# Three feed-forwards of a transformer stack: one whole gate and up tile each instead of two

## Chip, cores and metric

One core of one Trainium2 chip. The metric is device time in microseconds (us) of one execution of the program; the kernel before takes 2332.36 us (median of 3 runs, 2330.86 to 2334.24). The profile is of a further execution of its own, which took 2334.35 us; its span, from the first to the last instruction, is 2332.6 us.

## What is computed

A stack of three blocks on 512 tokens (with 16 meta tokens, 528 columns), width 1024, all in fp32: a mixer with sparse attention and retention, a feed-forward, a mixer with stick-breaking attention, a feed-forward, and a block of four parallel branches with its own feed-forward. The change concerns the three feed-forwards. Cut to them, the reference is:

```
def conv_ffn(h, w_up, w_gate, conv_w, conv_b, w_down):
    u = h @ w_up
    g = h @ w_gate
    g = causal_conv_of_width_3(g, conv_w) + conv_b
    return (jax.nn.silu(g) * u) @ w_down

# in the last block, without the convolution
act = silu(h @ w_gate) * (h @ w_up)
x = x + act @ w_down
```

`w_gate` and `w_up` are 1024 x 2816, which makes 22 tiles of 128 columns each; `w_down` is 2816 x 1024.

## The kernel before, in words

**Layout.** The residual stream lies transposed in SBUF as eight tiles `hT[k]` of 128 x 528 (features by tokens). A projection makes one 128-column tile of the result at a time: the weights are the stationary operand, the tokens move. fp32 is emulated by three passes: weights and activations are split into a high part (a cast to fp32r) and a low part (the rest), and each product is three matmuls, high x high, high x low and low x high. The high part of weights is cast on ScalarE (in some helpers on VectorE if that is free first), the low part is a subtraction on VectorE.

**Whole tiles.** `proj` (L689) multiplies a weight tile of 128 x 8 x 128 with the eight activation tiles: 8 x 3 matmuls per column range. The first feed-forward has two ranges of 264 columns; the second has two of 258 for the gate and one of 512 for up; the third has one of 512 for both. `wtile` (L663) loads a tile (512 KB, issued on SyncE's queue) into one of three places `w_raw` and splits it into `w_hi` and `w_lo`. `prefetch` (L659) does so at the end of the stage before, for tiles that the feed-forward will take first.

**Block products.** The class `Fast` (L1147) takes a gate tile and an up tile together as a 2 x 2 block problem (two halves of the 1024 features, two halves of the tokens) and computes it with seven block products in place of eight: 7 x 4 x 3 = 84 matmuls of half the tokens (264, 258 or 256 columns). For that it needs

- four sums of the activations for each of four feature pairs, made once at the start of each feed-forward (`Fast.__init__`, L1150: tiles `th`, `tl`, with temporary tiles in the ring of raw weights);
- sums of the weights, for each pair of tiles anew (`blocks`, L1193): two loads of 512 KB, `s13` (1024 elements a row), `s24` (two operations of 512), and four splits, three of 1024 and one of 512;
- sums of the products, seven VectorE operations and one ScalarE copy per pair (`pair`, L1228).

The raw weights, the high parts and the low parts go through rings of five places each (three `w_...`, two `s_...`); the whole tiles use the `w_...` places of the same rings.

**The feed-forward.** `ffn` (L1253) and `block2_ffn` (L1881) go over the 22 tiles in groups (of 4, 4, 4, 4, 3, 3 and of 5, 5, 5, 4, 3). `gate_up(f)` (L1278, L1891) makes the activation tile `f`: whole where `f < FS`, by block products otherwise, then convolution (in the first two), Silu, product, and the split of the result into `ah` and `al`. From the second group on, the down projection of the group before is spread between the tiles. So the first group has no down projection beside it. `FS` is 2 (L45).

```
                if f < FS:
                    proj(pall, wtile(f"w_gu{l}", 2 * f), x, times(g[:, 2:], r), grange)
                elif f in WHOLE[l]:
                    ...
                else:
                    u = fp.tile([P, gw], F32, name="u", bufs=1)
                    fast.pair(f, g[:, 2:], u, r)
```

`WHOLE` is empty. `prepare` (L192) lays the weights out by the same constant: `w_gu*` holds the `2 * FS` whole tiles, `w_gs*` the paired blocks of all others.

**What sets the order.** Operations are recorded, not issued: `Order.record` (L444) collects them with their dependencies and a cost, and `Order.flush` (L514), called at the end of each stage, emits them as a greedy list schedule: at each step the engine that is free first takes its ready operation with the best priority. The priority is the place in the program less a weighted length of the path behind the operation (`RANK`, L371); weight preparation inside `early` and `wtile` is moved ahead by 500 places. Every engine runs its operations in the order emitted, and nothing crosses a flush. All instructions are recorded by helpers, so the profile gives them one line (L502), and they are told apart by the tiles' names.

Of the kernel before, what the change touches and what calls it, by code (L numbers as in the profile page):

```python
# [41 lines left out]
OSP = 3  # L42
BST = 0
OB = 2
FS = 2  # L45
WHOLE = ((), (), ())
HS = S // 2

# [2 lines left out]
def pack(w, tiles):  # L51

    kt = w.shape[0] // P
    out = np.zeros((len(tiles), P, kt, P), w.dtype)
    r = w.reshape(kt, P, w.shape[1]).transpose(1, 0, 2)
    for i, parts in enumerate(tiles):
        for at, c0, n in parts:
            out[i, :, :, at:at + n] = r[:, :, c0:c0 + n]
    return np.ascontiguousarray(out.reshape(len(tiles), P, kt * P))


def paired(a, b):

    h = a.shape[2] // 2
    return np.stack([np.concatenate([b[:, :, h:], a[:, :, :h]], 2), np.concatenate([b[:, :, :h], a[:, :, h:]], 2)], 1)


def whole(c0, n):
    return [[(0, c0 + P * i, P)] for i in range(n // P)]
# [122 lines left out]
def prepare(i):  # L192
# [7 lines left out]
    for l in range(2):  # L200
        g, u = pack(i["ffn_w_gate"][l], whole(0, DFF)), pack(i["ffn_w_up"][l], whole(0, DFF))
        a[f"w_gu{l}"] = np.stack([g[:FS], u[:FS]], 1).reshape(2 * FS, P, D)
        a[f"w_gs{l}"] = paired(g[FS:], u[FS:]).reshape(-1, P, D)
        for n, (f0, f1) in enumerate(GROUPS):
# [9 lines left out]
    g, u = pack(i["w_gate_2"][0], whole(0, DFF)), pack(i["w_up_2"][0], whole(0, DFF))  # L214
    a["w_gu2"] = np.stack([g[:FS], u[:FS]], 1).reshape(2 * FS, P, D)
    a["w_gs2"] = paired(g[FS:], u[FS:]).reshape(-1, P, D)
    for n, (f0, f1) in enumerate(GROUPS2):
# [376 lines left out]
def body(ctx: ExitStack, tc, A, out):  # L594
# [64 lines left out]
    def prefetch(name, *tiles):  # L659
        for i in tiles:  # L660
            fetched[name, i] = wtile(name, i)

    def wtile(name, i, kt=KD):  # L663
        if (name, i) in fetched:
            return fetched.pop((name, i))
        n = kt * P
        O.shift -= 500
        raw = wp.tile([P, D], F32, name="w_raw", bufs=3)
        if (name, i) == ("w_even", 0):
            O.boost = 3e6  # L670
        dma(raw[:, :n], A[name][i])
        O.boost = 0.0
        hi = wp.tile([P, D], F32R, name="w_hi", bufs=3)
        lo = wp.tile([P, D], F32R, name="w_lo", bufs=3)
        split(raw[:, :n], hi[:, :n], lo[:, :n])
        O.shift += 500
        return v2(hi, P), v2(lo, P)
# [71 lines left out]
    class Following:  # L749
# [9 lines left out]
        def add(self, m):  # L759
            src = hT[m][:, self.c0:]  # L760
            h, l = split_scaled(src, self.gain(m), xp, KD, self.w)
            self.x[0].append(h)
            self.x[1].append(l)
            add_square(self.acc, m == 0, src, *self.args)
            if self.gain2 is not None:
                add_square(self.acc2, m == 0, src, *self.args, gain=self.gain2(m))
# [8 lines left out]
    def follow(*a, **k):  # L775
        nxt_[0] = Following(*a, **k)
        return nxt_[0].add
# [73 lines left out]
    def even_mixer():  # L851
        with ExitStack() as es:
# [270 lines left out]
                    add(m)  # L1123
            for m in range(RF, KD):
                add(m)
            prefetch("w_gu0", 0, 1, 2)
            O.flush()


# [17 lines left out]
    class Fast:  # L1147
# [45 lines left out]
        def blocks(self, f):  # L1193


            i = f - FS
            r1, r2 = self.load(A[self.name][2 * i]), self.load(A[self.name][2 * i + 1])
# [16 lines left out]
        def tile(self, f, n, evac, x, ranges):  # L1214

            i = f - FS
            if n == 0:
# [110 lines left out]
    def odd_mixer():  # L1328
# [8 lines left out]
        with ExitStack() as es:  # L1337
# [19 lines left out]
            def out_proj(n, k0, k1, add=None):  # L1357
                for m in range(KD):
                    proj(pall if add else pd, wtile(f"w_oo_{n}", m, k1 - k0), (o_hl[0][k0:k1], o_hl[1][k0:k1]), add_h(m),
                         ((Q0, 270), (270, 528)), boost=0.0 if add else BST)  # L1360
                    if add:
                        add(m)
# [117 lines left out]
                o_hl[1].append(l_)  # L1480
            out_proj(0, 0, OSP)
            out_proj(1, OSP, KD, follow(lambda m: gcol(3, m), Q0, op, "otmp", 2))
            prefetch("w_gu1", 0, 1, 2)
            O.flush()


# [2 lines left out]
    def block2_mixer():  # L1489
        with ExitStack() as es:  # L1490
# [384 lines left out]
            for m in range(KD):  # L1875
                proj(pall, wtile("w_mg", m), mgx, add_h(m, NM), ONE)
                add(m)
            prefetch("w_gu2", 0, 1, 2)
            O.flush()

    def block2_ffn():  # L1881
        with ExitStack() as es:
# [38 lines left out]
            O.flush()  # L1921

    steps = [even_mixer, lambda: ffn(0, 1), odd_mixer, lambda: ffn(1, 3), block2_mixer, block2_ffn]
    for step in steps:
        step()
# [14 lines left out]
```

## Time and profile before

| what | us |
|---|---|
| median of 3 runs | 2332.36 |
| lowest and highest run | 2330.86, 2334.24 |
| the profiled execution | 2334.35 |
| its span | 2332.6 |
| TensorE busy in the span | 2288.6 |
| VectorE busy | 2004.4 |
| ScalarE busy | 1184.2 |
| the first feed-forward, about | 435 to 800 |
| the second | 1097 to 1440 |
| the third | 1982 to 2332 |

The profile is one execution on the chip. Matmuls overlap, so the time that one of them takes in a steady stream is the step from start to start, not its own duration. An engine's idle time is put down to the instruction on another engine, or the load, that came last before it went on. `w_hi`, `w_lo`, `s_hi`, `s_lo` are split weights, `xh`, `xl` split activations, `th`, `tl` their split sums, `sp`, `sv`, `u`, `g` and `y` the intermediate results of a tile; `d`, `at` and `pv` are PSUM.

### The profile page before, as it was taken

What the parts mean: (1) busy time and instruction counts of PE and PEld (TensorE: products, weight loads), DVE (VectorE), ACT (ScalarE), POOL (GpSimd) and SP (SyncE); (2) the same over time, 40 slices, a digit from 0 to 9 for tenths busy, and PEclk for the clock granted to TensorE, in tenths of its full rate; (3) what the DMA queues carried; (4) which work ended last, traced back from release to release, by engine and by line L of the source; (5) the groups of instructions that cost most, each with busy time, mean ns of one, the idle gap of its engine ahead of it and who ended that gap; (6) DMA issues with size and microseconds to landing.
All of it is one profiled execution on the core that took longest, in us unless ns stands there. A gap on an engine that the chain in (4) does not pass through costs nothing.

```text
span 2332.6 us, 39795 instructions
## 1 busy us (share of the span) xinstructions
PE 2288.6 (98%) x15488; PEld 2094.2 (90%) x15488; DVE 2004.4 (86%) x3975; ACT 1184.2 (51%) x2183; POOL 0.2 (0%) x4
## 2 busy tenths in 40 slices
PE   7999999999999999999999999899999999999999
PEld 7999999989999999999899998677888788899998
DVE  6999898899998889998999998676898776998886
ACT  4423556544444578886444445243677622543442
POOL 0000000000000000000000000000000000000000
PEclk9999999999999999999999999999999999999999
DMA  6222222222332311102332333222222122333332
GB/s 202 72 65 73 80 78 65 96 91 95 97 106 94 93 58 53 55 28 74 113 108 88 109 99 108 89 71 84 84 86 80 53 84 95 106 112 98 112 99 82
DMA packets 75774, 206.09 MB, mean 88 GB/s; under 512 B 8996, under 2 KB 20720, under 8 KB 75584
## 3 DMA queue, kind: packets, MB, share of 16 engines
q1 hardware_dynamic: 75584, 203.53, 27.4%
q8 instruction: 122, 2.00, 0.4%
q14 instruction: 68, 0.56, 0.1%
HBM read 201.37 MB, written 6.84 MB: 89 GB/s over the span
## 4 chain that ended last, share of the span: by engine, by line
PE 92%; DVE 5%; DMA 2%; issue 1%; ACT 1%; SPq 0%; ACTq 0%; DVEq 0%
PE d L502 51%; PE at L502 33%; PE pv L502 8%; DMA w_raw<-w_even 1%; DVE w_lo L502 1%; DVE w_raw L502 1%; DVE s_lo L502 1%; DVE y L502 0%; DMA w_raw<-w_gu 0%; DVE s_raw L502 0%; ACT w_hi L502 0%; DMA h<-h 0%; DVE tl L502 0%; DMA ob<-c_oh 0%; DMA s_raw<-w_gs 0%
## 5 line engine op out<-in xcount | busy, mean ns | idle before, releaser
L502 PE MATMUL d<-xh,w_hi 128*128 128x264 f32 (+4 forms) x1616 | 480.8, 325 | 12.6 <-ACT w_hi L502 7.8
L502 PE MATMUL d<-xl,w_hi 128*128 128x264 f32 (+4 forms) x1616 | 482.2, 326 | 1.1 <-DVE xl L502 1.0
L502 PE MATMUL d<-xh,w_lo 128*128 128x264 f32 (+5 forms) x1616 | 477.7, 324 | 0.0
L502 DVE TENSOR_TENSOR w_lo<-w_raw,w_hi 128x1024 fp32r<-128x1024 f32 (+5 forms) x322 | 320.6, 998 | 45.5 <-ACT w_hi L502 32.6
L502 ACT CAST w_hi<-w_raw 128x1024 fp32r<-128x1024 f32 (+5 forms) x239 | 206.4, 865 | 301.3 <-PE d L502 178.8
L502 PEld LDWEIGHTS d<-xh,w_hi 128*128 128x128 f32 x1616 | 291.5, 190 | 39.2 <-ACT w_hi L502 8.3
L502 PEld LDWEIGHTS d<-xl,w_hi 128*128 128x128 f32 x1616 | 291.5, 190 | 24.9 <-DVE xl L502 2.3
L502 PEld LDWEIGHTS d<-xh,w_lo 128*128 128x128 f32 x1616 | 290.3, 190 | 23.5 <-issue 1.9
L502 ACT CAST s_hi<-w_raw 128x512 fp32r<-128x512 f32 (+3 forms) x112 | 90.7, 812 | 89.6 <-PE at L502 38.5
L502 DVE CAST w_hi<-w_raw 128x1024 fp32r<-128x1024 f32 (+3 forms) x83 | 49.2, 593 | 73.6 <-PE d L502 62.9
L502 DVE TENSOR_TENSOR s_lo<-w_raw,s_hi 128x512 fp32r<-128x512 f32 (+3 forms) x112 | 103.3, 927 | 10.0 <-ACT s_hi L502 8.7
L502 PE MATMUL at<-xh,s_hi 128*128 128x264 f32 (+2 forms) x356 | 101.6, 286 | 3.3 <-DVE y L502 1.3
L502 ACT CAST w_hi<-s_raw 128x1024 fp32r<-128x1024 f32 (+3 forms) x76 | 63.1, 832 | 81.9 <-PE at L502 29.4
L502 PE MATMUL at<-xh,s_lo 128*128 128x264 f32 (+2 forms) x356 | 101.2, 284 | 0.0
L502 PE MATMUL at<-xl,s_hi 128*128 128x264 f32 (+2 forms) x356 | 101.2, 284 | 0.0
L502 ACT CAST s_hi<-s_raw 128x1024 fp32r<-128x1024 f32 (+3 forms) x74 | 62.9, 852 | 57.7 <-PE at L502 27.6
L502 ACT ACTIVATE e<-e,m 128x256 f32<-128x256 f32 (+4 forms) x142 | 76.5, 550 | 14.8 <-DVE m L502 13.5
L502 PE MATMUL d<-th,s_hi 128*128 128x264 f32 (+2 forms) x284 | 80.8, 285 | 2.8 <-DVE sp L502 2.3
L502 PE MATMUL d<-th,s_lo 128*128 128x264 f32 (+2 forms) x284 | 80.9, 285 | 2.5 <-DVE s_lo L502 2.4
L502 PE MATMUL at<-al,w_hi 128*128 128x264 f32 (+1 forms) x256 | 81.5, 335 | 0.0
L502 PE MATMUL at<-ah,w_hi 128*128 128x264 f32 (+1 forms) x256 | 81.4, 335 | 0.0
L502 PE MATMUL at<-ah,w_lo 128*128 128x264 f32 (+1 forms) x256 | 81.2, 334 | 0.0
(684 smaller groups left out, 6823.4 us busy)
## 6 DMA issues: line engine op xcount, KB each, us to landing
w_raw<-w_gs SPq DMA_DIRECT2D x71, 512.0 KB, 3.7
w_raw<-w SPq DMA_DIRECT2D x59, 512.0 KB, 3.7
s_raw<-w_gs SPq DMA_DIRECT2D x49, 512.0 KB, 3.8
w_raw<-w_even SPq DMA_DIRECT2D x41, 512.0 KB, 3.6
w_raw<-w_odd SPq DMA_DIRECT2D x24, 512.0 KB, 3.7
w_raw<-w_dn SPq DMA_DIRECT2D x44, 256.0 KB, 2.6
s_raw<-w_dn SPq DMA_DIRECT2D x28, 256.0 KB, 2.5
w_raw<-w_eo SPq DMA_DIRECT2D x16, 384.0 KB, 3.0
```

The source lines that it names most:

```text
L502: return f(*[r(x) for x in a], **{n: r(x) for n, x in k.items()})
```

## The change

`FS` becomes 1: in each feed-forward the tile pair `f = 0` stays whole, and `f = 1` goes through the seven block products with all that follow. The weights of that pair move from `w_gu*` to `w_gs*` on the host, through `prepare`. The mixers' last lines prefetch the gate and the up tile of `f = 0` and no longer the gate tile of `f = 1`.

```
-FS = 2
+FS = 1
...
-            prefetch("w_gu0", 0, 1, 2)
+            prefetch("w_gu0", 0, 1)
...
-            prefetch("w_gu1", 0, 1, 2)
+            prefetch("w_gu1", 0, 1)
...
-            prefetch("w_gu2", 0, 1, 2)
+            prefetch("w_gu2", 0, 1)
```

## Rows read from the trace of the kernel before

**Rows 1.** The page, part 1: busy us, share of the span, instructions.

```profile
PE 2288.6 (98%) x15488; PEld 2094.2 (90%) x15488; DVE 2004.4 (86%) x3975; ACT 1184.2 (51%) x2183; POOL 0.2 (0%) x4
```

**Rows 2.** Stretches: length, busy us by engine, granted clock, DMA; feed-forwards' starts and rests.

```profile
438.00:506.00 68.00, 60.97 (x476) 58.17 (x475) 61.59 (x112) 34.09 (x52) 0.00 (x0) 1.00 0.30 97
506.00:800.00 294.00, 293.76 (x2413) 293.55 (x2413) 272.74 (x485) 134.11 (x189) 0.00 (x0) 1.00 0.31 97
1099.00:1163.00 64.00, 59.67 (x411) 54.64 (x410) 58.55 (x106) 33.98 (x53) 0.00 (x0) 0.97 0.30 98
1163.00:1440.00 277.00, 277.00 (x1885) 256.64 (x1884) 256.89 (x428) 125.29 (x178) 0.00 (x0) 1.00 0.31 98
1984.00:2022.00 38.00, 36.97 (x227) 32.58 (x226) 36.60 (x62) 22.61 (x35) 0.00 (x0) 1.00 0.33 111
2022.00:2300.00 278.00, 277.92 (x1943) 259.16 (x1942) 238.59 (x373) 114.12 (x156) 0.00 (x0) 1.00 0.32 102
```

**Rows 3.** TensorE's timeline: start, us, instruction, [idle before it <- what ended that].

```profile
435.33 0.28 PE L502 MATMUL at<-xh,w_hi 128*128 128x264 f32 x1
...
472.95 0.39 PE L502 MATMUL at<-xh,s_hi 128*128 128x264 f32 x1 [1.31 <-DVE g L502]
...
502.55 0.39 PE L502 MATMUL d<-th,s_hi 128*128 128x264 f32 x1 [2.27 <-DVE sp L502]
...
1132.47 0.48 PE L502 MATMUL at<-xh,s_hi 128*128 128x258 f32 x1 [1.34 <-DVE y L502]
```

**Rows 4.** The chain that ended last: start, us, what, matmuls in the piece.

```profile
541.25 3.04 PE d L502 x25
...
1121.97 2.53 PE d L502 x21
1132.47 2.86 PE at L502 x12
...
1873.45 63.14 PE d L502 x272
...
2082.40 2.75 PE d L502 x23
```

**Rows 5.** VectorE's timeline in the first feed-forward's start.

```profile
453.94 0.70 DVE L502 CAST w_hi<-w_raw 128x1024 fp32r<-128x1024 f32 x1 [2.98 <-DMA w_raw<-w_gu]
454.55 1.22 DVE L502 TENSOR_TENSOR w_lo<-s_raw,w_hi 128x1024 fp32r<-128x1024 f32 x1
455.69 1.22 DVE L502 TENSOR_TENSOR w_lo<-w_raw,w_hi 128x1024 fp32r<-128x1024 f32 x1
...
457.96 0.68 DVE L502 TENSOR_TENSOR s_lo<-w_raw,s_hi 128x512 fp32r<-128x512 f32 x1
458.56 0.68 DVE L502 TENSOR_TENSOR s_raw<-w_raw,s_raw 128x512 f32<-128x512 f32 x1
...
466.73 0.70 DVE L502 TENSOR_TENSOR y<-y,rrow 128x528 f32<-128x528 f32 x1
467.35 0.68 DVE L502 TENSOR_TENSOR w_raw<-w_raw,s_raw 128x512 f32<-128x512 f32 x1
467.95 0.42 DVE L502 TENSOR_TENSOR y<-at,y 128x264 f32<-128x264 f32 x1
468.30 0.42 DVE L502 TENSOR_TENSOR y<-d,y 128x264 f32<-128x264 f32 x1
```

**Rows 6.** SyncE's queue in the same start: issue, us, load.

```profile
445.44 0.33 SPq L502 DMA_DIRECT2D s_raw<-w_gs  x1
447.08 0.33 SPq L502 DMA_DIRECT2D w_raw<-w_gu  x1
447.70 9.56 SPq L502 DMA_DIRECT2D w_raw<-w_gs  x2
```

**Rows 7.** The page, part 6: loads of block weights, KB each, median us to landing.

```profile
w_raw<-w_gs SPq DMA_DIRECT2D x71, 512.0 KB, 3.7
```

**Rows 8.** A stretch of the second start, columns as in rows 2.

```profile
1130.00:1140.00 10.00, 8.20 (x56) 7.69 (x55) 8.31 (x16) 4.85 (x8) 0.00 (x0) 0.83 0.08 26
```

## The prediction

> **What bounds the kernel now.** I read the profile from the outside in. The page's engine shares come first [rows 1]: TensorE is busy 98% of the span and VectorE 86%, so work taken from TensorE counts, unless it is handed to a VectorE that is as full at that place. An average can't say that, so the next view is the table by stretches [rows 2], one row for the start of each of the three feed-forwards and one for the rest of it. The reader should see two regimes. In the rest of each feed-forward TensorE has no pause worth naming (0.2, 0.0 and 0.1 us) while VectorE idles 21, 20 and 39 us. In the starts TensorE lacks 68.00 - 60.97 = 7.0, 4.3 and 1.0 us, and VectorE has only 6.4, 5.5 and 1.4 us free out of 68, 64 and 38. Third, the waits on TensorE's own timeline [rows 3]: the pauses of the starts end on VectorE (the tiles g, sp and y). So VectorE sets the pace in the starts, TensorE everywhere else, and the change lies in the starts alone.
>
> **The change, part by part.** In each of the three feed-forwards the tile pair f = 1 stops being whole and becomes a block pair.
>
> TensorE. The pitch of a matmul comes from pieces of the chain of waits [rows 4]: 3.04/25 = 0.1216 us for 264 columns, 2.53/21 = 0.1205 for 258, 2.75/23 = 0.1196 for 256, 63.14/272 = 0.2321 for 512. The first feed-forward goes from 96 matmuls of 264 columns to 84: 12 x 0.1216 = 1.46 us less. In the second, 48 of 258 and 24 of 512 become 84 of 258: 24 x 0.2321 - 36 x 0.1205 = 1.23 us. In the third, 48 of 512 become 84 of 256: 11.14 - 10.05 = 1.09 us. In all 3.8 us less, although the number of matmuls rises by 36 (-12, +12, +36).
>
> VectorE. The prices are start-to-start steps on its timeline in the first start [rows 5]: 1.14 us for 1024 elements (454.55 to 455.69), 0.60 for 512, 0.62 for 528, 0.35 for 264 out of PSUM. A whole tile pair costs two low halves of weights and four PSUM results: 2 x 1.14 + 4 x 0.35 = 3.7 us. A block pair costs the weight sums (1.14 + 2 x 0.60 = 2.3), four low halves (3 x 1.14 + 0.60 = 4.0), seven PSUM operations (2.4) and one more product (0.6): 9.4 us. The convolution, the gate product and the split of the result stand in both. So 5.7 us more; with the widths of the second and third feed-forward it is 5.8 and 5.9. In all 17.4 us of VectorE work more, at the three places where VectorE has 6.4, 5.5 and 1.4 us free. A cast of 0.6 us that VectorE took over in the first start (453.94) may fall away; I leave it in the range.
>
> ScalarE. Four casts and one copy per block pair instead of two casts are some 2.1 us more, an estimate at VectorE's prices (1.14 + 0.60 + 0.35). It is busy 34 of 68 us there [rows 2], so I cost them at nothing; the VectorE work behind them covers them. Without that cover they would cost at most 3 x 2.1 = 6.3 us, which lies within the upper end below.
>
> DMA. Two loads of 512 KB per pair before and after. The third prefetch at the end of the stage before disappears, and with it the fourth load, which stood in the queue between the first block loads (issued at 447.08, between 445.44 and 447.70) [rows 6]. Its landing ended 2.98 us of VectorE idleness at 453.94 [rows 5]. After the change the second block load takes that place; two loads at 3.7 us each [rows 7] land near 452 instead of four by 457. The ring places that the sums of x occupy still hold both back, as 445.44 shows. Nothing else stands behind them in SyncE's queue.
>
> The cover. In the first feed-forward TensorE begins the first whole tile at 435.33 [rows 3]. Two whole pairs hold it for 192 x 0.1216 = 23.3 us, one for 11.7. With the norm's small matmuls it runs out of whole work near 450 instead of 462, while VectorE finishes the sums of x only around 450 and then has 6.3 us of sums and low halves for the first block pair. So I expect new TensorE waits of 2 to 3 us there. What is late next is VectorE's blocks for the second pair.
>
> The sum of a start. Where VectorE sets the pace, the end of the start moves by VectorE's added work less the idle time that it fills, and TensorE's saving becomes waiting. First start: 5.7 - 3.0 (the load's wait goes; the other 3.4 us wait for casts and matmuls and stay) = +2.7 us. Second: the 5.5 us free are waits on matmuls and on casts that waited for matmuls, and half of that should go when TensorE runs ahead of VectorE: 5.8 - 2.7 = +3.1. Third: only 1.4 us are free, but TensorE hardly waited, and each tile's last product and split (some 1.2 us on VectorE) are not needed before the down projection, so that part can slip: 5.9 - 1.4 - 2.3 = +2.2. Together +8.0 us.
>
> No row of the trace shows how much of a start's VectorE work can slip, so this is bounded. From below: everything hides and TensorE's saving counts, -3.8 us. From above: nothing hides, +17.4. I take +8.0, nearer the middle, because the third start has no long waits and the first loses a real one.
>
> Against the profiled execution's own 2334.35 us (span 2332.6 and 1.75 around it) the sum is 2342.4. That execution lies 2.0 us above the median of the runs, so the prediction for the median is 2340.4, 0.34% above 2332.36.
>
> **The clock, row against rule.** After a wait of 1.34 us that ended at 1132.47 [rows 3] twelve matmuls of 258 columns took 2.86 us, where twelve take 1.45 [rows 4]; the granted clock of that stretch is 0.83 of full [rows 8], so a part of it ran at 1.2 instead of 2.4 GHz. That drop cost 1.4 us. The longer wait before 502.55 (2.27 us) caused none: the first start has 1.00 [rows 2]. My sum therefore has no clock term. The Trainium skill, page TensorE: Matmul & The Clock Gate, section "HAM oscillation — how this bites in real kernels", says that gaps in the matmul stream bring TensorE's clock back to half and that the next burst starts slow. By that rule wider waits would add a drop at each start; one row agrees and one does not.
>
> **The rivals.**
> 1. The cover holds. VectorE's new work fits into its free time and into work that can wait until each feed-forward's rest, where it idles 80 us. It decides at the first starved block pair: if VectorE delivers the second block pair's low halves before TensorE has finished the first, nothing is lost and 3.8 us are won: 2330.6 in the profiled frame, 2328.6 as a median. Up to +2.5 us I count here. For it: 13 us free in the starts against 17 needed. Against it: those 13 us are scattered pieces that end on TensorE and ScalarE.
> 2. Full exposure. Nothing slips, because the results of f = 0 and 1 feed the same down projection: 2334.35 + 17.4 = 2351.8, median 2349.7. For it: VectorE's 61.59 of 68 us. Against it: a load's wait of 3.0 us that surely goes.
> 3. The clock drops at the two starts where it didn't: 2 x 1.4 = 2.8 on top of the forecast, median 2343.2. For and against: the two waits named above. That a drop comes at every start I put low; the Trainium skill's rule, named above, would have it so.
> 4. The new order is luckier. The order of work is a greedy one by priorities; with other operations it falls differently, and 12.3 us of TensorE waits lie in the starts. If it removed a third of them and kept the 3.8: -8 us, median 2324.5. Against it: those waits end on VectorE, which gets more to do.
>
> That the change does not do what it says I exclude: the weights' layout, the loop and the prefetches all go by the same constant.
>
> **How the numbers follow.** Differences of 0.2%, some 4.7 us, are about what a measurement of this kernel tells from no change. Forecast (+2.5 to +13): 0.50, of which 0.10 lies under +4.7. Cover holds (-3.8 to +2.5): 0.25. Full exposure (+13 to +17.4): 0.09. Clock drops: 0.06. Luckier order: 0.10. So faster 0.10, same 0.25 + 0.10 = 0.35, slower 0.40 + 0.09 + 0.06 = 0.55. The range goes from 2329.5 (into the case where the cover holds) to 2348.5 (into full exposure); what is left out is mostly the luckier order and the ends of both. The forecast's own range is 2334.9 to 2345.4.
>
> **What would show it.** In the new profile: TensorE's matmuls up by about 36; VectorE's busy time up by about 17 us from 2004.4 and ScalarE's by about 6; TensorE's idle time in the three starts up from 12.3 us to about 24, ended by low halves and sums of weights; a first new wait near 450 us in the first feed-forward; no wait for a load near 454; the rest of each feed-forward as busy as now. Wrong it would be if those starts end no later than now although VectorE has 5.7 us more in each: then VectorE's work could slip further than I think. It would also be wrong if the waits moved into the rests.

## The result and the profile after

The kernel after takes 2354.04 us (median of 4 runs, 2350.83 to 2356.02), the kernel before 2333.24 on the same chip (4 runs): 20.8 us slower, ratio 1.0083, 95% interval 1.0070 to 1.0095. Predicted were 2340.4 and at most 2348.5. The sign was right, the size was not: the loss is even above the 17.4 us at which nothing was to hide. All times compared below are of executions whose granted clock over the span was 0.989 to 0.996; one execution, of the kernel with four whole pairs (e5), took 2467.94 us at 0.848 and is compared with nothing. The profile after is of the run of 2356.02 us: its span is 2354.2, 21.6 more than the 2332.6 of the profile before, and sums read from the two profiles are set against 21.6.

The page of the profile after, part 1, answers to [rows 1]:

```profile
PE 2296.1 (98%) x15524; PEld 2102.1 (89%) x15524; DVE 2020.0 (86%) x4004; ACT 1195.4 (51%) x2193; POOL 0.2 (0%) x4
```

TensorE has its 36 matmuls more, VectorE 15.6 us more work (17 expected), ScalarE 11.2 (6 expected; it took casts that VectorE had done). So the change did what was costed, and the work added is of the size foreseen. The stretches, which answer to [rows 2] (same columns), show what was not:

```profile
436.00:510.00 74.00, 64.58 (x469) 61.73 (x468) 67.67 (x120) 39.14 (x59) 0.00 (x0) 0.93 0.30 97
510.00:803.00 293.00, 292.77 (x2405) 292.55 (x2404) 271.75 (x484) 132.72 (x187) 0.00 (x0) 1.00 0.31 97
1100.00:1180.00 80.00, 69.64 (x476) 63.87 (x476) 70.02 (x124) 40.59 (x61) 0.00 (x0) 0.94 0.28 90
1180.00:1460.00 280.00, 279.49 (x1884) 258.04 (x1882) 257.75 (x431) 128.62 (x185) 0.00 (x0) 1.00 0.31 99
2000.00:2040.00 40.00, 35.71 (x241) 32.99 (x240) 38.34 (x63) 23.91 (x35) 0.00 (x0) 0.91 0.38 119
2040.00:2320.00 280.00, 277.98 (x1941) 258.98 (x1940) 240.70 (x377) 113.05 (x154) 0.00 (x0) 1.00 0.32 101
```

The rests are nearly as busy as before (TensorE lacks 0.2, 0.5 and 2.0 us, where it lacked 0.2, 0.0 and 0.1). The starts lack more, 9.4, 10.4 and 4.3 us, and their granted clock, the third column from the end, has fallen from 1.00, 0.97 and 1.00 to 0.93, 0.94 and 0.91. TensorE's timeline after, cut to waits of the three starts (columns as in [rows 3]):

```profile
459.25 0.39 PE L502 MATMUL at<-xh,s_hi 128*128 128x264 f32 x1 [0.96 <-ACT s_hi L502]
461.98 0.59 PE L502 MATMUL d<-th,w_hi 128*128 128x264 f32 x1 [2.22 <-ACT w_hi L502]
...
1112.37 0.50 PE L502 MATMUL at<-xh,w_hi 128*128 128x512 f32 x1 [3.48 <-ACT rcol L502]
1130.45 0.58 PE L502 MATMUL d<-xh,s_lo 128*128 128x258 f32 x1 [2.22 <-DVE s_lo L502]
...
2009.83 0.39 PE L502 MATMUL d<-xh,w_hi 128*128 128x256 f32 x1 [1.90 <-ACT w_hi L502]
2011.51 0.58 PE L502 MATMUL d<-xh,w_lo 128*128 128x256 f32 x1 [1.18 <-DVE w_lo L502]
```

Four of these six end on ScalarE, which is half idle over the span. Its own timeline tells who was really late. The cast that ended the wait at 461.98 had waited for a weight sum of the second block pair (f = 2), which came at the end of a VectorE that did not pause from 448 to 462 us. At 1112.37 ScalarE itself was late: it had no pause from 1106.16 to 1112.32, with casts of the sums of x, a load of an activation table and, behind them, the two reads of the norm.

```profile
460.88 1.04 ACT L502 CAST w_hi<-w_raw 128x1024 fp32r<-128x1024 f32 x1 [1.69 <-DVE w_raw L502]
...
1110.10 1.28 ACT L502 ACT_TABLE_LOAD   x1
1111.40 0.26 ACT L502 ACTIVATE rcol<-at,c_small 128x4 f32<-128x4 f32 x1
1111.56 0.61 ACT L502 CAST th<-w_raw 128x516 fp32r<-128x516 f32 x1
1112.07 0.25 ACT L502 ACTIVATE rcol<-at,c_small 4x1 f32<-4x1 f32 x1
```

In the third start the weights were loaded, but VectorE was still at the sums of x (`tl`) and reached the low half of the first block load only behind them. VectorE's timeline there:

```profile
2009.04 0.69 DVE L502 TENSOR_TENSOR tl<-s_raw,th 128x512 fp32r<-128x512 f32 x1
2009.64 0.68 DVE L502 TENSOR_TENSOR g<-d,rrow 128x512 f32<-128x512 f32 x1
2010.24 1.22 DVE L502 TENSOR_TENSOR w_lo<-s_raw,w_hi 128x1024 fp32r<-128x1024 f32 x1
2011.37 0.68 DVE L502 TENSOR_TENSOR tl<-w_raw,th 128x512 fp32r<-128x512 f32 x1
```

Two windows laid on stretches that the trace records at half clock (columns as in [rows 2]):

```profile
461.40:468.20 6.80, 6.22 (x28) 6.22 (x29) 4.93 (x9) 1.44 (x3) 0.00 (x0) 0.50 0.48 154
2011.00:2017.80 6.80, 5.83 (x25) 5.54 (x26) 6.80 (x10) 5.23 (x8) 0.00 (x0) 0.50 0.47 154
```

At 0.50 of full, that is 1.2 GHz, 28 matmuls took 6.22 us, 0.222 each, where one of 264 columns takes 0.1216 otherwise [rows 4]: 28 x 0.10 = 2.8 us lost. The second window loses 25 x (0.233 - 0.1196) = 2.8 us as well. Each of them begins during one of the waits above.

**Where the loss is.** I take the 85 us from the first matmul of each feed-forward's norm as its start. The three of the kernel before, then the three of the kernel after:

```profile
439.60:524.60 85.00, 77.74 (x611) 74.72 (x610) 78.02 (x137) 42.27 (x63) 0.00 (x0) 1.00 0.31 100
1101.00:1186.00 85.00, 80.67 (x558) 74.29 (x557) 78.95 (x137) 43.02 (x65) 0.00 (x0) 0.98 0.31 100
1985.40:2070.40 85.00, 83.89 (x583) 77.54 (x582) 81.56 (x131) 44.56 (x64) 0.00 (x0) 1.00 0.34 113
...
437.60:522.60 85.00, 75.58 (x559) 72.73 (x558) 77.90 (x136) 44.19 (x66) 0.00 (x0) 0.94 0.30 96
1105.60:1190.60 85.00, 74.64 (x496) 67.73 (x495) 74.69 (x129) 42.97 (x65) 0.00 (x0) 0.94 0.29 91
1998.80:2083.80 85.00, 78.69 (x574) 74.47 (x573) 81.19 (x135) 43.93 (x63) 0.00 (x0) 0.96 0.32 103
```

There TensorE's idle time went from 7.3 + 4.3 + 1.1 = 12.7 us to 9.4 + 10.4 + 6.3 = 26.1: +13.4. The time at half clock follows from the granted clock: 0.06 below full is 0.12 of 85 us, that is 10.2. It went from 3.4 to 27.2 us; at 2.8 us lost in 6.8 that is 11.2 us, less the 1.4 of before: +9.8. TensorE's saving is -3.8. The sum is +19.4 of the 21.6 us between the two profiled executions. In another cut, each feed-forward from its norm to its last block product grew by 6.1, 11.0 and 8.0 us, and the other stages got 3.5 us shorter, 2.0 of them the stage that no longer ends with a third prefetch ahead of the first feed-forward; that makes the 21.6. The time at half clock differs between executions of one kernel: over their spans the four of the kernel after had 0.989 (2356.02, the profiled one, and 2354.66 us) and 0.993 (2353.42 and 2350.83), so for the median the 9.8 is rather too much.

### The profile page after: what moved, and what is told of

Its sections match the earlier page's. It is cut to its first block, busy times and chain, and to the rows that moved or that the text cites. A ratio compares the mean times of both kernels' runs of the same rounds, so it can differ in the third digit from the quotient of the medians.

```text
span 2354.2 us, 39896 instructions
## 1 busy us (share of the span) xinstructions
PE 2296.1 (98%) x15524; PEld 2102.1 (89%) x15524; DVE 2020.0 (86%) x4004; ACT 1195.4 (51%) x2193; POOL 0.2 (0%) x4
## 3 DMA queue, kind: packets, MB, share of 16 engines
q1 hardware_dynamic: 75584, 203.53, 27.2%
## 4 chain that ended last, share of the span: by engine, by line
PE 91%; DVE 5%; ACT 2%; DMA 2%; issue 1%; SPq 0%; DVEq 0%; ACTq 0%
PE d L502 51%; PE at L502 32%; PE pv L502 8%; DMA w_raw<-w_even 1%; DVE w_lo L502 1%; DVE w_raw L502 1%; DVE s_lo L502 1%; DVE y L502 1%; ACT w_hi L502 0%; DVE s_raw L502 0%; DVE g L502 0%; ACT th L502 0%; DMA h<-h 0%; SPq L502 0%; DVE h L502 0%
## 5 line engine op out<-in xcount | busy, mean ns | idle before, releaser
L502 PE MATMUL d<-xh,w_hi 128*128 128x264 f32 (+5 forms) x1684 | 498.7, 323 | 12.8 <-ACT w_hi L502 10.8
L502 PE MATMUL d<-xl,w_hi 128*128 128x264 f32 (+5 forms) x1684 | 500.5, 323 | 0.9 <-DVE xl L502 0.7
L502 ACT CAST s_hi<-w_raw 128x1024 fp32r<-128x1024 f32 (+3 forms) x115 | 87.9, 770 | 93.4 <-PE at L502 41.2
L502 DVE TENSOR_TENSOR s_lo<-w_raw,s_hi 128x1024 fp32r<-128x1024 f32 (+3 forms) x115 | 99.8, 875 | 8.5 <-ACT s_hi L502 7.1
L502 PE MATMUL at<-xh,w_hi 128*128 128x264 f32 (+3 forms) x284 | 83.2, 294 | 4.5 <-ACT rcol L502 4.3
L502 PE MATMUL at<-xl,w_hi 128*128 128x264 f32 (+3 forms) x284 | 83.2, 293 | 0.0
L502 PE MATMUL at<-xh,w_lo 128*128 128x264 f32 (+3 forms) x284 | 83.1, 292 | 0.1
L502 DVE TENSOR_TENSOR w_lo<-s_raw,w_hi 128x1024 fp32r<-128x1024 f32 (+3 forms) x79 | 75.9, 964 | 7.7 <-ACT w_hi L502 6.6
L502 DVE TENSOR_TENSOR s_lo<-s_raw,s_hi 128x512 fp32r<-128x512 f32 (+1 forms) x77 | 68.8, 900 | 7.6 <-ACT s_hi L502 6.8
L502 PE MATMUL d<-th,w_hi 128*128 128x264 f32 (+2 forms) x240 | 69.7, 290 | 5.2 <-ACT w_hi L502 2.9
```

The costliest lines, as they stand in the source:

```text
L502: return f(*[r(x) for x in a], **{n: r(x) for n, x in k.items()})
```

## The experiments

The theory from here: the added VectorE work makes TensorE wait in each start by itself, and the waits bring the clock down, which costs nearly as much again. The rivals: it is the dropped prefetch; the cover is too short whatever VectorE has to do; the order merely fell badly. The table puts the results together. "Idle" and "half clock" are TensorE's in the three starts of 85 us; each time is set against the median of the kernel before that ran beside it (2333.24 to 2334.94).

| kernel | us | against before | idle us | half clock us |
|---|---|---|---|---|
| before | 2333.24 | | 12.7 | 3.4 |
| after | 2354.04 | +20.8 | 26.1 | 27.2 |
| e1: first feed-forward alone | 2339.24 | +4.3 | 15.6 | 10.2 |
| e2: no weight sums | 2337.30 | +2.4 | 17.9 | 6.8 |
| e3: after with extra matmuls | 2344.18 | +9.2 | 16.2 | 0 |
| e4: three whole pairs | 2322.78 | -12.2 | 2.4 | 0 |
| e5: four whole pairs | 2327.87 | -6.2 | 1.0 | 0 |
| e6: before with extra matmuls | 2338.51 | +4.5 | 6.0 | 3.4 |
| e7: before, two prefetched | 2339.95 | +5.9 | 15.6 | 13.6 |
| e8: after, sums on GpSimd | 2352.38 | +18.3 | 26.4 | 13.6 |
| e9: after, block prefetched | 2348.49 | +15.2 | 23.8 | 20.4 |
| e10: three whole, two prefetched | 2330.76 | -2.6 | 9.1 | 10.2 |

Before, after, e4, e5 and e9 are medians of several runs; the others ran once. Runs of one kernel lie up to 3.6 us from their median (e9), most within 2.5, so a difference of a few us between two kernels that ran once is not shown by the times alone. A difference of two kernels can be taken from their times or from the third column, and the two ways differ by up to 1.7 us.

**e1: the change in the first feed-forward alone.** Set against the kernel after:

```
-FS = 1
+FSL = (1, 2, 2)
...
-            prefetch("w_gu1", 0, 1)
+            prefetch("w_gu1", 0, 1, 2)
...
-            prefetch("w_gu2", 0, 1)
+            prefetch("w_gu2", 0, 1, 2)
```

> One whole tile pair in the first feed-forward, two in the other two. Theory (each start pays by itself: VectorE's added work makes TensorE wait, and the waits halve TensorE's clock): only the first start gets longer, by 6 us, the stage before ends some 2 us earlier, and the whole is 4 us above the kernel before, about 2337; the second and third feed-forward stay as they were. Rival (the cost is not local, the new order of work disturbs what follows): the second and third feed-forward move too, and the whole is 10 us or more above.

Measured: 2339.24 us, +4.3. The first feed-forward takes 345.8 us from its norm to its last block product, as in the kernel after (345.7; before 339.6), the second and third took -1.2 and +1.4 against before, and the stage ahead of the first ends 2.5 us earlier. The stretches of its three starts:

```profile
437.10:522.10 85.00, 75.39 (x558) 72.54 (x557) 77.87 (x135) 44.16 (x66) 0.00 (x0) 0.94 0.30 96
1104.50:1189.50 85.00, 80.95 (x568) 74.39 (x567) 80.01 (x140) 44.10 (x66) 0.00 (x0) 1.00 0.31 100
1988.90:2073.90 85.00, 83.10 (x570) 76.31 (x569) 80.09 (x130) 43.87 (x62) 0.00 (x0) 1.00 0.34 113
```

Only the changed start has more idle time than before (9.6 us for 7.3; the others have 4.1 for 4.3 and 1.9 for 1.1) and a clock under 1.00. So for the first start the cost is local, and no accident of the whole order.

**e2: block products without the weight sums.** For f = 1 the sums `s13` and `s24` are left out, and the two loads' own splits stand in for theirs, so this kernel computes something else with the same matmuls. Set against the kernel after:

```
+            if f == FS:
+                w1, w2 = self.halves(r1), self.halves(r2)
+                return part(w1, 1), part(w2, 1), part(w1, 0), part(w1, 0), part(w2, 0), part(w1, 1), part(w2, 0)
```

> The changed kernel, but the block products of tile pair f = 1 take the loaded weights as they are: the sums of the weights are left out, and two splits take the place of four. That takes 4.0 of the 5.7 us that VectorE got more per start, two casts, and the chain load, sum, cast, low half; all matmuls and loads stay. Theory (VectorE's work and its chain hold TensorE): TensorE's idle time in the starts falls by 10 us or more, the half-rate stretches go with it, and the time is 2335 to 2342. Rival (one whole pair is too short a cover for the sums of the activations and the loads, whatever VectorE does with the weights): the first waits of each start stay, and the time stays above 2348.

Measured: 2337.30 us, 16.7 under the kernel after. The sums and the two splits hanging on them make most of the loss, as the theory has it. Its starts:

```profile
437.80:522.80 85.00, 78.76 (x610) 76.17 (x609) 80.41 (x142) 46.22 (x69) 0.00 (x0) 0.98 0.33 106
1099.60:1184.60 85.00, 79.14 (x568) 72.86 (x567) 79.63 (x140) 44.78 (x66) 0.00 (x0) 1.00 0.32 106
1982.50:2067.50 85.00, 79.18 (x583) 74.89 (x582) 79.09 (x131) 44.04 (x64) 0.00 (x0) 0.98 0.33 104
```

The idle time fell by 8.2 us (26.1 to 17.9), under the 10 expected, and the time at half clock by 20.4, which is 8.4 us at the price above: 16.6 together. But 6.8 us at half clock are left, and the first waits of the second and third start stayed nearly what they are in the kernel after. TensorE's timeline:

```profile
1105.81 0.50 PE L502 MATMUL at<-xh,w_hi 128*128 128x512 f32 x1 [2.93 <-ACT rcol L502]
...
1993.54 0.39 PE L502 MATMUL d<-xh,w_hi 128*128 128x256 f32 x1 [1.90 <-ACT w_hi L502]
```

These two come before any weight sum is wanted. The rival of the short cover holds for them, though not its time of 2348 or more.

**e3 and e6: extra matmuls ahead of the first block products.** 32 matmuls per start whose results are overwritten, in the kernel after (e3) and in the kernel before (e6); the same lines in both.

```
+            if f == FS:
+                x = nxt_[0].x[0][0]
+                for ps in (c11, q, q2, s_):
+                    for _ in range(8):
+                        T.matmul(ps, x[:, :P], x[:, :w], start=True, stop=True, skip_group_check=True)
             self.times(c11, a11, self.b[0][0], True)
```

> The changed kernel with 32 extra matmuls on the banks of pair f = 1 ahead of its products (8 on each of four results, which the real products then overwrite): 3.8 us more matmul work per start, to be done while TensorE waits. Theory (the lowered clock is a cost of its own, some 10 us): time at the lower clock in the three starts falls from 27 us to under 10, and the kernel gains 4 to 8 us although it does more, 2346 to 2350. Rival (the clock only falls where TensorE would have waited anyway): no gain, or 3 to 10 us more, 2354 to 2364.

> The kernel before (two whole pairs) with the same 32 extra matmuls per start ahead of its first block products, whose results are not used. It has only one half-rate stretch of 3.4 us in the starts. If in the kernel after the extra matmuls paid because they kept the clock up (the theory), they can give back at most 1.7 us here and cost up to 3 x 3.9 us where TensorE didn't wait: 2333 to 2345. If they paid by the other order of the work that they bring, or by something else that any start has, the time falls here as well, by 5 us or more.

Measured: e3 2344.18 us, 9.9 us less than the kernel after although TensorE has 96 matmuls (11.6 us at the pitches of the prediction) more to do. Its starts:

```profile
439.20:524.20 85.00, 78.00 (x612) 74.91 (x611) 80.69 (x143) 45.70 (x67) 0.00 (x0) 1.00 0.31 103
1102.70:1187.70 85.00, 80.01 (x580) 74.46 (x579) 81.07 (x141) 45.92 (x68) 0.00 (x0) 1.00 0.31 103
1987.70:2072.70 85.00, 80.75 (x609) 76.63 (x608) 81.94 (x136) 43.88 (x63) 0.00 (x0) 1.00 0.31 103
```

The granted clock is 1.00 in all three. The account closes: 11.6 us of work, less 9.9 us of idle time that it fills (26.1 to 16.2), less the 11.2 us that the clock had cost, is -9.5. In e6 the same matmuls cost 2338.51 - 2334.05 = 4.5 us: 11.6 less 6.7 of filled idle time (12.7 to 6.0), with the time at half clock unchanged, is +4.9. So they don't pay by themselves or by another order; they pay where there is a clock to keep up. The clock is a cost of its own, about 10 us of the 20.8.

**e4 and e5: more whole pairs.** The opposite of the change, set against the kernel before:

```
-FS = 2
+FSL = (3, 3, 3)
...
```

(and the same with 4 in each; the three prefetches of the kernel before)

> The other way: three whole tile pairs in each feed-forward, TensorE 3.8 us more than in the kernel before, VectorE 17 us less. Theory (the starts wait for VectorE): the 12.3 us that TensorE waits in the starts of the kernel before, and its 3.4 us at the lower clock, shrink to 4 us or less, so 2324 to 2330. Rival (those waits don't depend on how much VectorE has to do): the matmuls' 3.8 us come on top, 2336 to 2338.

> Four whole pairs in each feed-forward. With three, the starts have 2.4 us of TensorE idle time left and no stretch at half rate, so by the theory (waits on VectorE, and the clock that falls in them) there is nothing left to win: the fourth whole pair costs the matmul time that block products save, 1.46 + 1.23 + 1.09 = 3.8 us, and the time is about 2326 (2324.5 to 2327.5 beside a kernel before of about 2335). Rival: VectorE's relief still pays, in the rests too; then it is no higher than 2322.

Measured: e4 2322.78 us (2320.76 to 2324.38), ratio to before 0.9952, interval 0.9935 to 0.9968: better than both kernels, although it does 3.8 us more of matmuls than the kernel before. Its starts:

```profile
439.00:524.00 85.00, 83.10 (x676) 82.24 (x675) 77.60 (x139) 44.96 (x67) 0.00 (x0) 1.00 0.33 102
1093.30:1178.30 85.00, 85.00 (x581) 78.21 (x580) 79.80 (x139) 42.61 (x64) 0.00 (x0) 1.00 0.33 107
1972.20:2057.20 85.00, 84.48 (x548) 76.29 (x546) 77.06 (x123) 43.12 (x62) 0.00 (x0) 1.00 0.36 113
```

TensorE lacks 2.4 us in all; most of what was 12.7 us of waiting is work. The columns explain some 8 us of the gain (10.3 of idle time and 1.4 of clock, less 3.8 of matmuls); the other 4 are not accounted for. With four whole pairs there is nothing left to fill, and e5 goes up again to 2327.87 (ratio 0.9973, interval 0.9963 to 0.9984), just above its expected range: 5.1 us over e4, or 6.0 by the third column, where the matmuls alone say 3.8. Three is the best of the four values; the step from three to two costs 12 us, from two to one 21.

**e7: the dropped prefetch alone.** The kernel before, with its two whole pairs, and two prefetched tiles. Set against the kernel before:

```
-            prefetch("w_gu0", 0, 1, 2)
+            prefetch("w_gu0", 0, 1)
```

(and the same for the two others)

> The kernel before (two whole pairs) without the third prefetch at the end of the stage before: the smaller part of the change alone. Theory: the block pair for f = 1 brings the loss, so this part alone costs or gains no more than 2 us: 2332 to 2337 beside about 2335. Rival: the work moved out of the stage before is a good part of the loss: 2340 or more.

Measured: 2339.95 us, +5.9. My theory lost this one: I had left this part of the change at 2 us at most. Against before, the feed-forwards took -1.5, +2.2 and +7.2 us. TensorE's timeline in the third start, and the stretch after the waits:

```profile
1994.54 0.39 PE L502 MATMUL at<-xh,w_hi 128*128 128x256 f32 x1 [1.90 <-ACT w_hi L502]
1996.22 0.58 PE L502 MATMUL at<-xh,w_lo 128*128 128x256 f32 x1 [1.17 <-DVE w_lo L502]
```

```profile
1995.50:2005.70 10.20, 8.93 (x25) 7.10 (x26) 8.97 (x12) 4.00 (x6) 0.00 (x0) 0.50 0.46 151
```

These are the waits of the kernel after, 1.90 and 1.18, in a kernel without a block pair for f = 1: TensorE has used up its prefetched tiles and wants the high and then the low half of the next from a ScalarE and a VectorE that are still at the sums of x. The idle time of this start grew by 2.6 us only; most of the rest of the 7.2 is the clock, at 0.50 for the next 10.2 us (4.2 us at the price above).

**e8: the weight sums on GpSimd.** Set against the kernel after:

```
-            V.tensor_tensor(two(s13), two(r2)[:, 0:1, :].to_broadcast([P, 2, 512]), two(r1), op=ALU.add)
+            E = G if f == FS else V
+            E.tensor_tensor(two(s13), two(r2)[:, 0:1, :].to_broadcast([P, 2, 512]), two(r1), op=ALU.add)
...
```

> The kernel after, with the weight sums of f = 1 (one operation of 1024, two of 512) on GpSimd instead of VectorE. Nothing in the trace shows what GpSimd takes for one. If VectorE's amount of work sets the pace, its relief of 2.3 us per start comes back once or more (with the clock): 2336 to 2348. If the chain load, sum, split, product sets it (the rival), slower sums make the first block products later still: 2356 or more.

Measured: 2352.38 us, between the two expectations. GpSimd's timeline (columns as in [rows 5]) shows what the sums take there:

```profile
449.71 2.43 POOL L502 TENSOR_TENSOR w_raw<-w_raw,s_raw 128x1024 f32<-128x1024 f32 x1 [449.26 <-DMA w_raw<-w_gs]
452.21 1.62 POOL L502 TENSOR_TENSOR s_raw<-w_raw,s_raw 128x512 f32<-128x512 f32 x1
453.91 2.16 POOL L502 TENSOR_TENSOR s_raw<-s_raw,w_raw 128x512 f32<-128x512 f32 x1
```

The three sums take 6.2 us there, where VectorE takes 2.3: VectorE is relieved by 2.3 us and the chain to the first products is 3.9 longer. TensorE's idle time stayed (26.4 us for 26.1), which doesn't tell amount from chain; this run left the question open. Taking the sums off VectorE was worth nothing in idle time where they came later for it.

**e9: a third prefetch for the kernel after.** The first block load of f = 1 is fetched and split at the end of the stage before, and loaded again for the sums. Set against the kernel after:

```
             prefetch("w_gu0", 0, 1)
+            prefetch("w_gs0", 0)
... (and the same for w_gs1 and w_gs2)
-            w1, w24, w13 = self.halves(r1), self.halves(s24), self.halves(s13)
+            w1 = wtile(self.name, 0) if f == FS else self.halves(r1)
+            w24, w13 = self.halves(s24), self.halves(s13)
```

> The kernel after with a third prefetch again: at the end of the stage before, the first block load of f = 1 is fetched and split, and it is loaded a second time in the feed-forward for the sums. Theory as it now stands: a part of the loss is the dropped third prefetch, which in the third start leaves TensorE without split weights (waits of 1.90 and 1.18 us that two_prefetched shows too) and lets the clock fall. Then the third feed-forward, 324.7 us from its norm to its last block product, comes down to 320 or less with no half-rate stretch, and the time is 2342 to 2350. Rival: the block pair alone makes the loss, by its VectorE work and its chain: 2352 to 2357, and 323 to 326 us in the third.

Measured: 2348.49 us (2344.91 to 2349.69), ratio 1.0058, interval 1.0041 to 1.0074. The total is in the theory's range, +15.2 against +20.8, each beside its own runs of before, but the place is not: the third feed-forward took 325.9 us (324.7 in the kernel after), the second came down from 338.1 to 329.5. So in the kernel after, too, the missing prefetch is worth some 5.6 us (20.8 less 15.2), and it is the second feed-forward that gets them back. TensorE's timeline in the third start:

```profile
2004.98 0.58 PE L502 MATMUL d<-xh,s_hi 128*128 128x256 f32 x1 [3.62 <-ACT s_hi L502]
```

The wait on the first split (1.90 and 1.18) has gone and come back in one piece at the next product, which needs a weight sum. In the third start the dropped prefetch and the block pair therefore each suffice to open the same gap; their costs don't add.

**e10: two prefetched tiles with three whole pairs.** e4 with the shorter prefetches of e7.

> Three whole pairs, two prefetched tiles in place of three: against three whole pairs (2322.8, some 11 us under the kernel before) the prefetch alone. Theory: 4 to 7 us more, 2326.5 to 2330 beside a kernel before of 2334, most of it in the third start, with waits of about 1.9 and 1.2 us on split weights and a half-rate stretch behind them. Rival: with more whole work behind it the order finds something else to run and the prefetch is worth under 2 us: 2321 to 2325.

Measured: 2330.76 us, 8 us over e4 (10.0 between the profiled executions), a little more than expected. The feed-forwards grew against e4 by 0.7, 4.5 and 7.2 us, and the third start has the same picture (TensorE's timeline, then the stretch that holds it):

```profile
1988.54 0.79 PE L502 MATMUL d<-xh,w_hi 128*128 128x512 f32 x1 [4.18 <-DVE w_hi L502]
1990.27 0.80 PE L502 MATMUL d<-xh,w_lo 128*128 128x512 f32 x1 [0.52 <-DVE w_lo L502]
```

```profile
1987.50:1994.30 6.80, 5.25 (x12) 3.67 (x13) 6.08 (x7) 3.24 (x5) 0.00 (x0) 0.50 0.74 235
```

More whole work behind the gap doesn't close it. What closes it is whole work whose split weights are there before the feed-forward begins.

## Why the prediction was wrong, and where it was right

**Right: what bounds.** VectorE sets the pace in the starts, TensorE in the rests. Nearly all of the loss is in the starts; the rests lack 2.8 us in all, and the 2.0 of the third lie within the first 85 us after its norm.

**Right: the work.** TensorE +36 matmuls, VectorE +15.6 us for 17.4, ScalarE +11.2 for 6.

**Near in size, but by luck: the VectorE sum.** The starts' idle time was to go from 12.3 to about 24 us; it is 26.1. With TensorE's saving that is +9.6, against the forecast of +8.0. By places it missed: I gave +2.7, +3.1 and +2.2, and in the same terms they are +0.7, +4.8 and +4.1. The misses cancelled in part.

**The step that failed: "My sum therefore has no clock term".** It carried about half of the loss. I had two waits before me, 1.34 us with a drop and 2.27 without, and let them cancel. The rival that the clock drops at the two other starts had the right mechanism, a price of 2.8 us and a chance of 0.06. In the kernel after it was not one short drop per start: 10.2, 10.2 and 6.8 us at half clock, in time lost some 10 us more than before (e3 takes them away and gets them back). Adding those to the sum gives the measured time nearly: 8.0 + 9.8 = 17.8 of 20.8. The 17.4 us that I had set as the upper end, with nothing hidden, was no bound for the same reason: it had no clock in it. The rule that the prediction cites from the Trainium skill, page TensorE: Matmul & The Clock Gate, section "HAM oscillation — how this bites in real kernels" (gaps bring the clock to half, and the next burst starts slow), has the side of it that my sum lacked; the rows at 0.50 agree with it in direction.

**The second step that failed: the third prefetch.** I counted it as a gain of 3.0 us in the first start and as nothing elsewhere. In the first start that was about right: e7 ends the stage before 1.9 us earlier and the feed-forward takes 1.5 less, and VectorE waits for no load near 454 (ScalarE's cast at 455.69 waited 1.62 us for one of the second pair's loads). But the prefetched gate tile was also the work that carried TensorE over the sums of x. Under "The cover" I worked that out for the first feed-forward alone. The new waits of 2 to 3 us near 450 were 0.72 us at 451.69 and 0.21 at 454.12; the 2.22 us at 461.98 are the second block pair's, which I had named as late next without a price. I did not work the cover out for the second and third, where it is dearer: 3.48 us at 1112.37, where TensorE's next tile waits for the PSUM bank that the norm holds until `rcol` is read, and 3.1 us near 2010. For the third start I argued that TensorE "hardly waited", hence +2.2. It was +8.0, and e7 shows +7.2 of it without any block pair.

**ScalarE** was costed at nothing behind VectorE. Its casts end many of the waits. At 460.88 it had itself waited 1.69 us for VectorE, and there the step holds. At 1112.37 it does not: ScalarE had no pause for 6 us, and the reads of the norm came last in its order. The casts ahead of them are those of the sums of x, which the kernel before has too (there the reads ran from 1105.15 to 1106.08, while TensorE still had the third prefetched tile), so this wait is the cover's price again and not that of the block pair's casts; e7 has it without the block pair (3.44 us at 1103.51). No run took ScalarE's share away alone.

**What stays open.** Why the clock fell after some gaps and not after others of the same length, and how much of the block pair's own idle time is VectorE's amount of work and how much the length of the chain load, sum, cast, low half, product (e8 doesn't tell). Nor did a run move the loads alone: the second pair's were issued at 451.83 and 452.44, and one of them ended ScalarE's wait of 1.62 us at 455.69.

## What to carry to other kernels

Where the engine that feeds TensorE is full at the start of a stage, as VectorE was here, cheaper matmuls that need more preparation can be a loss there: keep the first tiles plain, as many as it takes to cover the preparation (three pairs here, 12 us better than two), and prepare the first of them in the stage before. Price a new TensorE gap at its length plus the clock: here 13.4 us of added idle time brought a further loss of about 10 us by the clock. A prefetch that seems to serve a small load may be the cover of something else; drop it alone on paper, start by start, before counting it as a gain.

## What the runs showed of the hardware that was not expected

- The amount of idle time doesn't tell whether the clock falls. e8's first start has 9.9 us of idle time at a granted clock of 1.00, the kernel after 9.4 us at 0.94 (its row stands with the 85 us above). e8's row:

```profile
437.80:522.80 85.00, 75.10 (x577) 70.90 (x576) 81.91 (x138) 45.52 (x67) 6.20 (x3) 1.00 0.31 103
```

- Useless matmuls can make a kernel faster: with 96 of them (11.6 us of work) e3 is 9.9 us faster than the kernel after.
- GpSimd took 2.43 us for a sum of 1024 elements a row and 1.6 to 2.2 for one of 512; VectorE takes 1.22 and 0.69 for the same.
